# A decoder layer on one Trainium2 core: the last two pairs of feature tiles finish the tokens' second half first, the last norm and the stores of y go by halves, and the norm's columns and the operand loads are joined in

## The chip, the core and the metric

The kernel runs on one core of one Trainium2 chip. The metric is the device time of one execution in microseconds. Three executions of the kernel before took 2793.79, 2793.49 and 2789.72 us; the median is 2793.49.

In the tables PE is TensorE (PEld its weight loads), DVE is VectorE, ACT is ScalarE, POOL is GpSimd and SP is SyncE, which only issues DMAs. GpSimd and ScalarE issue DMAs too, each on a queue of its own.

## What is computed

One step of a hybrid decoder layer and the final norm. The part that matters here, cut from the reference:

```python
def block(x, rg_h, rg_conv, C, n, m, ml_conv, mk, mv, w):
    y, new = mixer(rmsnorm(x, w['g_mix']), rg_h, rg_conv, C, n, m, ml_conv, w)   # ends in y @ w_out
    x = x + y.astype(x.dtype)
    x = x + cross_attn(rmsnorm(x, w['g_xattn']), mk, mv, w).astype(x.dtype)      # q = h @ w_cq, ..., o @ w_co
    hf = rmsnorm(x, w['g_ffn'])
    x = x + (jnp.square(jax.nn.relu(hf @ w['w_up'])) @ w['w_down']).astype(x.dtype)
    return x, new

y_prompt = rmsnorm(xp, g_final)
y_sample = rmsnorm(xs, g_final)
```

x has 2048 features. 512 prompt tokens and 8 sampled tokens go through together, 520 in all. w_up is 2048 x 8192 and w_down 8192 x 2048. All is float32.

## The kernel before, in words

**Layout.** Features lie on the 128 partitions, so x is 16 feature tiles of 128 x 520. The tokens are cut into two halves of 260 (HALF, HT = 260). A matmul has a 128 x 128 block of weights and 260 tokens.

**Products.** Each operand is split into a high and a low part that TensorE multiplies exactly enough, and one product of parts is three matmuls (high by high, high by low, low by high). The projections w_out, w_cq, w_co, w_up and w_down are done by Strassen's scheme. A unit is a pair of feature tiles of the output, and its 2 x 2 blocks are (first or second tile) by (first or second token half). A unit takes seven products p0 to p6 of 24 matmuls each (`product`, L943, matmuls L955). Products go to three PSUM banks: p0, p2, p4 and p6 to acca, p1 and p5 to accc, p3 to accb. acca is carried on from p2 through p4 to p6. After each product VectorE adds the bank to a block of x (`onto`, L958, addition L962), or in the up stage ScalarE copies it out (L973) and VectorE adds (L971). The order of the blocks for p0 to p6 is (0,0), (1,1), (0,1), (0,0), (1,1), (0,1), (1,0): tile, then token half.

**Weights.** Raw weight blocks are loaded on SyncE's queue (`fetch`, L889, seven buffers) some products ahead. `prep` two products ahead (LOOK) forms sums of blocks on VectorE (L834), casts the high part on ScalarE (whi, L101) and takes the low part on VectorE (wlo, L102).

**Operands.** The right-hand sides are seven combinations of token data. They are built unit by unit at the end of the stage before (`mixed`), spilled to DRAM on GpSimd's queue (`spill`, L845: tdcq, tdup, tdd) and read back (`batch_load`, L856: the load L858 on SyncE's queue, the cast of the high part L859 on ScalarE, the low part L854 on VectorE). Each of the seven sets has two loads, of 520 KB and, for cq and up, 390 KB; the missing column block of these is built on chip (`set_tail`, L874).

**The stages in order.** Input projection and mixer, out (8 units), keys, cq (8), attention, co (8), up (32), then w_down in four groups d0 to d3 of 8 units each. x itself goes through DRAM between stages (dx_0 to dx_7 of four copies): co stores its x on GpSimd's queue (L995), up scales it back and stores it again (`scale_back`, L1323: loads L1341, multiplications L1345, stores L1346), and down loads it (`down_load`, L1362). In d3 all eight pairs stay in SBUF.

**scale_back.** Norm factors are kept apart from x. At the start of up they are inverted twice (`negative_inverse`, L1316: Ln on ScalarE, Exp, then two VectorE operations; each Ln and each Exp comes with a table load), and x is multiplied by the result.

**The last norm** (`final`, L1388). The squares of every x tile are summed into ss as the units of d3 end (L1385, L1386). After the last product, four matmuls by ones sum ss over the partitions, the factor r of all 520 tokens is computed over the full 128 x 520 (Ln, Exp, one correction step), and VectorE (L1413, eleven tiles) and GpSimd (L1411, five tiles, whose gain ScalarE multiplied in, L1392) multiply x by it. Sixteen stores of a full tile follow, alternately on the queues of SyncE and ScalarE (L1415).

**What sets the order.** A scheduler places the instructions of each engine by the order of the code and by priorities: the weight preparation and fetches have high priority, the evacuation of a product the next. Generators (`start`, `step_tasks`) advance by some steps with each product. In d3 the units run in order, but for 0 and 1, whose products alternate (`pairs`).

Of the kernel before, what the change touches and what calls it, by code (L numbers as in the profile page):

```python
# [17 lines left out]
P = 128  # L18
# [27 lines left out]
def tile_trunk(ctx: ExitStack, tc: tile.TileContext, a, o):  # L46
# [751 lines left out]
    def rest():  # L798
# [57 lines left out]
        def batch_load(key, s, b, n=4):  # L856
            hi, lo = op_tile(), op_tile()
            load(lo[:, 0:n].bitcast(F32), td[key][b][:, s, 0:n])  # L858
# [55 lines left out]
        def strassen(key, n, src, evac, enter_=None, leave=None, left=None, pairs=(), hooks={}):  # L914
# [12 lines left out]
            for u, p in order:  # L927
                k, box = base + u, boxes[u]
                job = dict(unit=k, q=p, kind=1, cost=0.55 if key == "cq" else 0.2, prep=lambda k=k, p=p: weights(k, p),
# [13 lines left out]
        def product(key, p, w, box):  # L943
            bank, _, s = ORDER[p]
            new = p in (0, 1, 3)
# [366 lines left out]
        def up_enter():  # L1312
            enter("d", x=2, r=1, t=2, w=2)()
            start(scale_back())
# [33 lines left out]
        def up_evac(u, p, box):  # L1348
# [11 lines left out]
        X = []  # L1360

# [8 lines left out]
        def down_evac(u, p, box, last):  # L1370
            onto([st["X", u][:, 0], st["X", u][:, 1]], p, box["out"])
            if p == 6 and not last:
                store(dx[3][u], st["X", u])
            if last and p == 6:
                for n in (2 * u, 2 * u + 1):
                    if n == 0:
                        st["sc2"] = op_tile((P, T), F32)
                        V.scalar_tensor_tensor(out=st["sc2"], in0=scl, scalar=1.0 / D, in1=scl,
                                               op0=ALU.mult, op1=ALU.mult)
                        st["ss"] = tl("ss", (P, T))  # L1380
                        S.activation(st["ss"], X[n], AF.Square)
                    else:
                        for c in HALF:
                            sq = ax()[:, 0:HT]
                            S.activation(sq, X[n][:, c], AF.Square)  # L1385
                            V.tensor_tensor(out=st["ss"][:, c], in0=sq, in1=st["ss"][:, c], op=ALU.add)  # L1386

        def final():  # L1388

            r, v, s_, q_ = (op_tile((P, T), F32) for _ in range(4))  # L1390
            for n in range(2, KB, 3):
                S.activation(X[n], X[n], AF.Copy, scale=pc(C_FIN, n))  # L1392
            for c in HALF:
# [263 lines left out]
```

## Time and profile before

| | us |
|---|---|
| median of three executions | 2793.49 |
| the profiled execution's own time | 2796.05 |
| its span | 2794.2 |
| last product of co ends, first product of up starts | 1409.9, 1411.7 |
| first unit of up ends | 1465.7 |
| last product of d3 ends | 2768.7 |
| first store of y issued | 2779.3 |

A time in the views is counted from the start of the span. A row of the timeline gives the start, the duration, the engine, the line of the code, the operation with its names (written by, read from), its shape and count, and in brackets how long the engine stood idle before it and what ended that. A group has the busy time, the mean of one in ns, and the idle time before. The table of windows gives for each stretch the busy time of each engine and in brackets the number of instructions.

### The profile page before, as it was taken

What the parts mean: (1) busy time and instruction counts of PE and PEld (TensorE: products, weight loads), DVE (VectorE), ACT (ScalarE), POOL (GpSimd) and SP (SyncE); (2) the same over time, 40 slices, a digit from 0 to 9 for tenths busy, and PEclk for the clock granted to TensorE, in tenths of its full rate; (3) what the DMA queues carried; (4) which work ended last, traced back from release to release, by engine and by line L of the source; (5) the groups of instructions that cost most, each with busy time, mean ns of one, the idle gap of its engine ahead of it and who ended that gap; (6) DMA issues with size and microseconds to landing.
All of it is one profiled execution on the core that took longest, in us unless ns stands there. A gap on an engine that the chain in (4) does not pass through costs nothing.

```text
span 2794.2 us, 52079 instructions
## 1 busy us (share of the span) xinstructions
PE 2665.4 (95%) x21146; PEld 2613.6 (94%) x21146; DVE 2245.1 (80%) x3203; ACT 1437.9 (51%) x2114; POOL 107.5 (4%) x164
## 2 busy tenths in 40 slices
PE   8999999999999999889969999999999999999996
PEld 8999999999999998669969999999998999999996
DVE  7777788658887898789878777777878887978886
ACT  6445556525455467675455455545554353434543
POOL 0000000030000000000000000000000000000000
PEclk9999999999999999999989999999999999999998
DMA  4666643377676579976666545454457465654632
GB/s 169 196 211 213 196 148 94 99 272 275 220 247 227 202 229 324 335 256 210 198 216 228 174 145 168 151 162 157 159 198 258 164 238 168 222 186 161 223 109 81
DMA packets 178857, 551.24 MB, mean 197 GB/s; under 512 B 23725, under 2 KB 33645, under 8 KB 178617
## 3 DMA queue, kind: packets, MB, share of 16 engines
q1 hardware_dynamic: 152808, 453.61, 48.9%
q0 software_dynamic: 24080, 90.50, 9.0%
q8 instruction: 166, 2.72, 0.4%
q10 hardware_dynamic: 1728, 3.80, 0.4%
q14 instruction: 75, 0.61, 0.1%
HBM read 427.45 MB, written 120.51 MB: 196 GB/s over the span
## 4 chain that ended last, share of the span: by engine, by line
PE 36%; issue 16%; DMA 4%; DVE 2%; ACT 2%; POOL 1%; SPq 0%; POOLq 0%; DVEq 0%; ACTq 0%
PE acca L955 19%; PE accc L955 9%; PE accb L955 5%; PE mv L1202 2%; PE ax L185 1%; DMA op<-dq 1%; DMA x<-dx 1%; DMA dx<-x 1%; DVE wlo L102 1%; DVE op L854 0%; DMA kv<-in_V 0%; ACT kv L1159 0%; PE row L1129 0%; DMA tdup<-w 0%; DMA op<-tdup 0%
## 5 line engine op out<-in xcount | busy, mean ns | idle before, releaser
L955 PE MATMUL acca<-op,whi 128*128 128x260 f32 x5632 | 1037.3, 285 | 33.2 <-ACT t L973 10.3
L955 PEld LDWEIGHTS acca<-op,whi 128*128 128x128 f32 x5632 | 877.7, 190 | 38.1 <-ACT whi L101 11.9
L955 PE MATMUL acca<-op,wlo 128*128 128x260 f32 x2816 | 801.9, 285 | 4.5 <-DVE wlo L102 4.4
L101 ACT CAST whi<-raw 128x1024 fp32r<-128x1024 f32 x388 | 406.8, 1050 | 426.7 <-PE acca L955 148.8
L955 PEld LDWEIGHTS acca<-op,wlo 128*128 128x128 f32 x2816 | 535.4, 190 | 6.1 <-DVE wlo L102 6.1
L102 DVE TENSOR_TENSOR wlo<-raw,whi 128x1024 fp32r<-128x1024 f32 x388 | 473.5, 1222 | 77.4 <-ACT whi L101 73.7
L955 PE MATMUL accc<-op,whi 128*128 128x260 f32 x2816 | 518.5, 284 | 1.4 <-ACT whi L101 1.3
L101 ACT CAST whi<-raws 128x1024 fp32r<-128x1024 f32 x264 | 276.9, 1049 | 369.2 <-PE accc L955 110.0
L166 PE MATMUL mm<-xa,whi 128*128 128x260 f32 x2624 | 432.9, 286 | 11.1 <-ACT whi L101 8.3
L955 PEld LDWEIGHTS accc<-op,whi 128*128 128x128 f32 x2816 | 438.1, 189 | 2.7 <-ACT whi L101 1.8
L102 DVE TENSOR_TENSOR wlo<-raws,whi 128x1024 fp32r<-128x1024 f32 x264 | 322.9, 1223 | 121.5 <-ACT whi L101 120.8
L955 PE MATMUL accc<-op,wlo 128*128 128x260 f32 x1408 | 400.2, 284 | 0.9 <-DVE wlo L102 0.9
L166 PEld LDWEIGHTS mm<-xa,whi 128*128 128x128 f32 x2624 | 365.0, 190 | 13.7 <-ACT whi L101 8.3
L955 PE MATMUL accb<-op,whi 128*128 128x260 f32 x1408 | 262.1, 286 | 8.4 <-ACT op L859 4.6
L955 PEld LDWEIGHTS accc<-op,wlo 128*128 128x128 f32 x1408 | 266.5, 189 | 1.3 <-DVE wlo L102 1.2
L166 PE MATMUL mm<-xa,wlo 128*128 128x260 f32 x1312 | 266.2, 284 | 0.0
L955 PEld LDWEIGHTS accb<-op,whi 128*128 128x128 f32 x1408 | 219.6, 190 | 9.8 <-ACT op L859 4.8
L166 PEld LDWEIGHTS mm<-xa,wlo 128*128 128x128 f32 x1312 | 203.9, 190 | 0.7 <-DVE wlo L102 0.5
L955 PE MATMUL accb<-op,wlo 128*128 128x260 f32 x704 | 200.8, 285 | 0.4 <-DVE wlo L102 0.3
L854 DVE TENSOR_TENSOR op<-op,op 128x1040 fp32r<-128x1040 f32 (+3 forms) x136 | 159.9, 1180 | 36.5 <-ACT op L859 22.0
L859 ACT CAST op<-op 128x1040 fp32r<-128x1040 f32 (+1 forms) x112 | 111.9, 1007 | 90.1 <-DMA op<-tdd 55.0
L101 ACT CAST whi<-wraw 128x1024 fp32r<-128x1024 f32 x82 | 85.5, 1043 | 122.8 <-PE mm L166 99.9
(386 smaller groups left out, 3355.0 us busy)
## 6 DMA issues: line engine op xcount, KB each, us to landing
raw<-in_w_up SPq DMA_DIRECT2D x128, 512.0 KB, 3.4
raw<-in_w_down SPq DMA_DIRECT2D x100, 512.0 KB, 4.1
wraw<-in_w_in SPq DMA_DIRECT2D x79, 512.0 KB, 4.0
tdd<-w POOLq DMA_DIRECT2D x32, 1040.0 KB, 6.3
x<-dx SPq DMA_DIRECT2D x56, 520.0 KB, 5.5
op<-tdd SPq DMA_DIRECT2D x56, 520.0 KB, 5.2
dx<-x POOLq DMA_DIRECT2D x48, 520.0 KB, 4.9
raw<-in_w_mk SPq DMA_DIRECT2D x32, 512.0 KB, 5.3
```

Source lines behind the costliest of these rows:

```text
L101: S.copy(hi, raw)
L102: V.tensor_tensor(out=lo, in0=raw, in1=hi.bitcast(F32), op=ALU.subtract)
L166: PE.matmul(ps[:, hf, 0:HT], w[:, j, :], x[:, HALF[hf]], start=(k == 0 and wi == 0), stop=(k == n - 1 and wi == 2))
L185: PE.matmul(out, u, v, start=first and i == 0, stop=last and i == 2)
L854: V.tensor_tensor(out=lo, in0=src, in1=hi.bitcast(F32), op=ALU.subtract)
L859: S.copy(hi[:, 0:n], lo[:, 0:n].bitcast(F32))
L955: PE.matmul(out, u[:, k], x[:, j], start=(new and k == 0 and i == 0), stop=(k == 7 and i == 2), skip_group_check=not new)
L1202: PE.matmul(st["mv"][i], x[:, ms], u[:, j], start=(k == 0 and wi == 0), stop=(k == KB - 1 and wi == 2))
```

## The change

The change has four parts.

1. `batch_load` issues the operand loads of cq and up on GpSimd's queue (store) in place of SyncE's (load).
2. `scale_back` is started after the last activation of unit 2 of up, in place of the stage's start; its first norm read (`mean_of`) still stands early.
3. In d3 the last two units (6 and 7) run p0, p1, p2, p4, p5 of each, then p3 of both, then p6 of both. With p5 the second token half of both units is complete. p6 gets a bank of its own, and what p4 had carried on into it is added to block (1,0) after p4. The fetch distances of these units follow.
4. The last norm runs by token halves (`final(1)` after p5 of unit 7, `final(0)` after its p6). The factor is computed on columns, tokens on partitions (`pieces`), with a square root in place of Ln and Exp; the columns of the scales are made after unit 0, where the table of the root is loaded too. Gains are multiplied in on ScalarE for units 0 to 5 (`gained`). Each half stores eight 128 x 2 x 260 pieces.

```diff
         def batch_load(key, s, b, n=4):
             hi, lo = op_tile(), op_tile()
-            load(lo[:, 0:n].bitcast(F32), td[key][b][:, s, 0:n])
+            (store if key in ("cq", "up") else load)(lo[:, 0:n].bitcast(F32), td[key][b][:, s, 0:n])
...
             for u in range(n):
-                if u in pairs:
+                if u == halves_:
+                    order += [(v, p) for v in (u, u + 1) for p in (0, 1, 2, 4, 5)]
+                    order += [(v, p) for p in (3, 6) for v in (u, u + 1)]
+                elif halves_ is not None and u == halves_ + 1:
+                    pass
+                elif u in pairs:
...
-            new = p in (0, 1, 3)
+            new = p in (0, 1, 3) or (p == 6 and "late" in box)
...
         def up_enter():
             enter("d", x=2, r=1, t=2, w=2)()
-            start(scale_back())
...
         def scale_back():
-            for _ in range(16):
-                yield
             va, vb = tl("x", (P, 2, T)), tl("x", (P, 2, T))
             v, y, t = va[:, 0], va[:, 1], vb[:, 0]
+            st["rphi"] = tl("r", (P, T))
+            with tc.issue_after(st["mark"].ins):
+                negative_inverse(y, t, scl)
             mean_of(v)
-            st["rphi"] = tl("r", (P, T))
-            negative_inverse(y, t, scl)
...
-                S.activation(w[:, 0:4], t, AF.Square)
+                ins = S.activation(w[:, 0:4], t, AF.Square)
+                if u == 2:
+                    st["mark"] = ins
+                    start(scale_back())
...
         def down_evac(u, p, box, last):
-            onto([st["X", u][:, 0], st["X", u][:, 1]], p, box["out"])
+            Xu = [st["X", u][:, 0], st["X", u][:, 1]]
+            onto(Xu, p, box["out"])
+            if p == 4 and "late" in box:
+                onto(Xu, 6, box["out"])
...
+            if last and p == 6 and u == 0:
+                ps = ax()
+                pieces(ps, [scl], ident, 0)
+                pieces(ps, [scl], ident, 1)
+                pieces(ps[:, 6:12], [esc], ident, 0)
+                pieces(ps[:, 6:12], [esc], ident, 1)
...
+                ins = S.activation(st["ss"], X[0], AF.Square)
+                with tc.issue_after(ins.ins):
+                    S.activation(cols[:, 3], ones[:, 0:6], AF.Sqrt)
+                square(Xu[1], HALF)
+                gained(u)
+            elif last and p == 6 and "late" not in box:
+                for x in Xu:
+                    square(x, HALF)
+                gained(u)
+            elif last and p == 5 and "late" in box:
+                for x in Xu:
+                    square(x, HALF[1:])
+                if u == 7:
+                    final(1)
+            elif last and p == 6:
+                square(Xu[0], HALF[:1])
+                if u == 7:
+                    sq = op_tile((P, HT), F32)
+                    S.activation(sq, Xu[1][:, HALF[0]], AF.Square)
+                    final(0, sq)
+                else:
+                    square(Xu[1], HALF[:1])
...
+        def pieces(ps, ts, col, h):
+            for c, cs in ((0, PIECES[0]), (1, PIECES[1]), (2, PIECES[0]), (2, PIECES[2])):
+                n = cs.stop - cs.start
+                for i, t in enumerate(ts):
+                    o_ = (h * HT if t.shape[-1] == T else 0) + cs.start
+                    PE.matmul(ps[0:n, 3 * h + c:3 * h + c + 1], t[:, o_:o_ + n], col[:, 0:1],
+                              start=(i == 0), stop=(i == len(ts) - 1))
+
+        def final(h, more=None):
+            c3 = slice(3 * h, 3 * h + 3)
+            v, s_, q_, rc = (cols[:, 3 + i, c3] for i in range(4))
+            ps = ax()
+            pieces(ps, [st["ss"]] + ([] if more is None else [more]), ones, h)
+            V.tensor_tensor(out=v, in0=ps[:, c3], in1=st["sc2"][:, c3], op=ALU.mult)
+            V.tensor_tensor(out=v, in0=v, in1=st["esc"][:, c3], op=ALU.add)
+            S.activation(s_, v, AF.Sqrt)
+            V.reciprocal(s_, s_)
...
+            rp = ax()[:, 0:HT]
+            for c, cs in enumerate(PIECES):
+                n = cs.stop - cs.start
+                PE.matmul(rp[:, cs], rc[0:n, c:c + 1].to_broadcast([n, P]), ident[0:n, 0:n],
+                          start=True, stop=True)
+            r = op_tile((P, HT), F32)
+            S.copy(r, rp)
+            for i, u in enumerate((1, 0, 3, 2, 5, 4, 6, 7)):
+                x = st["X", u][:, :, HALF[h]]
+                if u > 5:
+                    for j in range(2):
+                        V.scalar_tensor_tensor(out=x[:, j], in0=x[:, j], scalar=pc(C_FIN, 2 * u + j), in1=rp,
                                                op0=ALU.mult, op1=ALU.mult)
+                elif u % 2:
+                    V.tensor_tensor(out=x, in0=x, in1=rp[:, None, :].to_broadcast([P, 2, HT]), op=ALU.mult)
+                else:
+                    G.tensor_tensor(out=x, in0=x, in1=r[:, None, :].to_broadcast([P, 2, HT]), op=ALU.mult)
+                (S.dma_start if i % 2 else load)(o["y"][2 * u:2 * u + 2, :, HALF[h]].rearrange("n p t -> p n t"), x)
...
-                     pairs=(0,) if last else (0, 6),
+                     pairs=(0,) if last else (0, 6), halves_=6 if last else None,
...
-        final()
         stage["stack"].close()
+        axs.close()
```

Three places show how the instructions move. The first is the start of the up stage. On SyncE's queue before, loads of raw weights (raw, from w_up) and of operands (op, from tdup) stand in turn, and x of `scale_back` follows:

```order
L889 DMA raw_16546<-in_w_up 128x1024
L858 DMA op_16334<-tdup_120 128x1040
L858 DMA op_16339<-tdup_121 128x780
L889 DMA raw_16607<-in_w_up 128x1024
L858 DMA op_16373<-tdup_120 128x1040
L858 DMA op_16378<-tdup_121 128x780
L858 DMA op_16412<-tdup_120 128x1040
L889 DMA raw_16736<-in_w_up 128x1024
L858 DMA op_16417<-tdup_121 128x780
L858 DMA op_16464<-tdup_120 128x1040
L858 DMA op_16469<-tdup_121 128x780
L1341 DMA x_17310<-dx_0_146 128x1040
```

On GpSimd's queue now, the operand loads stand behind the last spill of w and the store of dx_7, the last x of co:

```order
L1004 DMA dx_6_152<-x_15971 128x1040
L845 DMA tdup_121<-w_16159 1024x1x260
L858 DMA op_16213<-tdup_121 128x780
L858 DMA op_16252<-tdup_120 128x1040
L858 DMA op_16257<-tdup_121 128x780
L858 DMA op_16291<-tdup_120 128x1040
L1004 DMA dx_7_153<-x_16204 128x1040
L858 DMA op_16296<-tdup_121 128x780
L858 DMA op_16334<-tdup_120 128x1040
L858 DMA op_16339<-tdup_121 128x780
L858 DMA op_16373<-tdup_120 128x1040
L858 DMA op_16378<-tdup_121 128x780
```

SyncE's queue holds raw weights alone there; the eight x loads of `scale_back` (now L1348) stand between raw loads of units 3 to 6.

The second place is ScalarE at the start of up: before, the two table loads and activations of the first inverse stand among the operand casts, and the same four rows come again after the last of these casts.

```order
L874 CAST op_16295<-w_16452 128x260
L1318 ACT_TABLE_LOAD
L1318 ACTIVATE x_17036<-scl 128x520
L1319 ACT_TABLE_LOAD
L1319 ACTIVATE x_17036<-x_17036 128x520
L101 CAST whi_16513<-raws_16421 128x1024
L859 CAST op_16295<-op_16296 128x780
```

Now both stand among the weight casts (whi) of unit 3; the copies t (now L982) take products out of PSUM:

```order
L101 CAST whi_17239<-raw_17061 128x1024
L1326 ACT_TABLE_LOAD
L1326 ACTIVATE x_17198<-scl 128x520
L1327 ACT_TABLE_LOAD
L1327 ACTIVATE x_17198<-x_17198 128x520
L101 CAST whi_17274<-raw_16998 128x1024
L982 COPY t_17233<-accc_17248 128x260
L101 CAST whi_17306<-raws_17152 128x1024
L982 COPY t_17233<-acca_17208 128x260
L101 CAST whi_17336<-raw_17000 128x1024
L1326 ACT_TABLE_LOAD
```

The third place is ScalarE at the end: od holds the norm's columns, ax_31221 the factor of the second half, L1428 and L1420 are squares of x, and L1478 the stores of y.

```order
L101 CAST whi_31275<-raw_30918 128x1024
L1454 ACTIVATE od<-od 128x3
L1428 ACTIVATE ax_31331<-x_30775 128x260
L1467 COPY op_31225<-ax_31221 128x260
L1478 DMA out_y<-x_29386 128x2x260
L1478 DMA out_y<-x_29776 128x2x260
L1478 DMA out_y<-x_30307 128x2x260
L1478 DMA out_y<-x_30980 128x2x260
L1428 ACTIVATE ax_31334<-x_30775 128x260
L1428 ACTIVATE ax_31363<-x_30980 128x260
L1420 ACTIVATE op_31366<-x_30980 128x260
L1454 ACTIVATE od<-od 128x3
```

The four stores of the second half stand ahead of the last three squares of the first. On TensorE the four column matmuls of the second half stand behind the third matmul of p3 of unit 7, and its three broadcasts behind the first matmul of p6 of unit 6; the eight and three of the first half come last.

More of the change, by code (lines that the diff above doesn't have):

```diff
@@ L928, in strassen @@
                 k, box = base + u, boxes[u]
-                job = dict(unit=k, q=p, kind=1, cost=0.55 if key == "cq" else 0.2, prep=lambda k=k, p=p: weights(k, p),
+                late = halves_ is not None and u >= halves_
+                if p == 0 and late:
+                    box["late"] = True
+                job = dict(unit=k, q=p, kind=1, late=late, far=5 if late and u > halves_ else 7, cost=0.55 if key == "cq" else 0.2, prep=lambda k=k, p=p: weights(k, p),
                            run=lambda w, p=p, box=box: product(key, p, w, box),
@@ new lines, in square, with gained @@
+        def square(x, cs):
+            for c in cs:
+                sq = ax()[:, 0:HT]
+                S.activation(sq, x[:, c], AF.Square)
+                V.tensor_tensor(out=st["ss"][:, c], in0=sq, in1=st["ss"][:, c], op=ALU.add)
+        def gained(u):
+            for n in (2 * u, 2 * u + 1):
+                S.activation(X[n], X[n], AF.Copy, scale=pc(C_FIN, n))
+        PIECES = [slice(0, CH), slice(CH, 2 * CH), slice(2 * CH, HT)]
+        def pieces(ps, ts, col, h):
[5 more added lines that the diff above has]
+                              start=(i == 0), stop=(i == len(ts) - 1))
@@ L1494, in rest @@
         NEED = (0, 1, 1, 3)
+        LATE = (0, 1, 1, 5)
         fetches = [[] for _ in seq]
```

58 lines of the change are left out of this document (15 added, 43 removed).

## The prediction, made before the changed kernel ran

> **What bounds the kernel now.** I read the page first, then busy time by stretches of 10 to 20 us, then the timeline and the chain of waits wherever TensorE stood still.
>
> ```profile
> span 2794.2 us, 52079 instructions
> PE 2665.4 (95%) x21146; PEld 2613.6 (94%) x21146; DVE 2245.1 (80%) x3203; ACT 1437.9 (51%) x2114; POOL 107.5 (4%) x164
> ```
>
> TensorE is busy for 95% of the span, so an edit beside its work is worth nothing, and only the places where it waits can give time. Two of these lie in the change's reach: the start of the up stage and the end. Here are stretches of the windows view: width, then busy time of PE, PEld, DVE, ACT and POOL, granted clock, DMA share, GB/s. The first is a steady co unit, the next five the start of up, the last the stores of y.
>
> ```profile
> 1340.00:1360.00 20.00, 20.00 (x169) 20.00 (x168) 17.55 (x23) 9.67 (x11) 1.41 (x2) 1.00 0.63 200
> 1410.00:1420.00 10.00, 7.07 (x56) 6.87 (x57) 9.80 (x14) 8.34 (x13) 0.55 (x1) 1.00 0.74 293
> 1420.00:1430.00 10.00, 4.50 (x26) 3.75 (x26) 8.15 (x10) 9.45 (x12) 0.00 (x0) 0.85 0.40 146
> 1430.00:1440.00 10.00, 5.35 (x23) 5.05 (x23) 8.97 (x12) 4.24 (x6) 0.00 (x0) 0.63 0.55 199
> 1440.00:1450.00 10.00, 2.96 (x13) 2.97 (x14) 7.86 (x12) 5.64 (x10) 0.00 (x0) 0.54 0.50 186
> 1450.00:1461.00 11.00, 7.92 (x62) 7.52 (x60) 5.66 (x9) 5.25 (x6) 0.54 (x1) 0.96 0.42 146
> 2780.00:2794.20 14.20, 0.00 (x0) 0.00 (x0) 5.91 (x9) 0.00 (x0) 4.21 (x4) 0.50 0.80 300
> ```
>
> From 1410 to 1461 VectorE is the busiest engine (40.4 of 51 us, the five windows added), and it has holes of its own. What made them stands in the timelines and the chain. The first two rows are TensorE's last matmul of co and its longest stall; then SyncE's queue, ScalarE and VectorE; the last three, without a queue's name, are links of the chain.
>
> ```profile
> 1409.60 0.28 PE L955 MATMUL accc<-op,wlo 128*128 128x260 f32 x1
> 1447.04 0.80 PE L955 MATMUL acca<-op,whi 128*128 128x260 f32 x2 [10.08 <-ACT t L973]
> 1439.15 0.33 SPq L889 DMA_DIRECT2D raw<-in_w_up  x1
> 1439.58 1.33 SPq L858 DMA_DIRECT2D op<-tdup  x3
> 1443.71 0.84 ACT L859 CAST op<-op 128x780 fp32r<-128x780 f32 x1 [3.52 <-DMA op<-tdup]
> 1448.02 1.28 ACT L1318 ACT_TABLE_LOAD   x1
> 1449.31 0.64 ACT L1318 ACTIVATE x<-x 128x520 f32<-128x520 f32 x1
> 1458.55 2.04 DVE L1345 TENSOR_TENSOR x<-x,r 128x520 f32<-128x520 f32 x3 [3.30 <-DMA x<-dx]
> 1440.06 5.26 DMA op<-tdup
> 1453.40 5.12 DMA x<-dx
> 1460.98 4.68 PE acca L955 x24
> ```
>
> The last three operand loads stand on SyncE's queue behind a weight load (raw, L889) that waited for a free buffer until 1439.15; they were issued from 1439.58 and the last landed at 1445.3. ScalarE's casts waited for them, the copy t (L973) waited behind the casts, and TensorE waited 10.08 us for that copy. Then the last product waited for a VectorE addition queued behind L1345, which waited 5.12 us for x<-dx. The first unit of up thus ran from 1409.9 to 1465.7, 56 us; the steady row above has 20.00 of 20 us busy with 169 matmuls, and a unit is seven products of 24 matmuls: about 20 us, 2.9 a product. Some 36 us are lost here.
>
> The tail, from the timeline:
>
> ```profile
> 2768.75 0.43 DVE L962 TENSOR_TENSOR x<-acca,x 128x260 f32<-128x260 f32 x1 [1.56 <-PE acca L955]
> 2769.21 0.70 ACT L1385 ACTIVATE ax<-x 128x260 f32<-128x260 f32 x2 [1.72 <-DVE x L962]
> 2770.12 1.15 PE L1395 MATMUL ax<-ss,ones 128*128 128x260 f32 x4 [1.41 <-DVE ss L1386]
> 2773.15 1.28 ACT L1399 ACT_TABLE_LOAD   x1
> 2777.86 0.60 ACT L1407 COPY rp<-op 128x520 f32<-128x520 f32 x1 [2.11 <-DVE op L1403]
> 2777.97 6.25 POOL L1411 TENSOR_TENSOR x<-x,op 128x520 f32<-128x520 f32 x5 [175.28 <-DVE op L1403]
> 2778.49 7.42 DVE L1413 SCALAR_TENSOR_TENSOR x<-x,par,rp 128x520 f32<-128x520 f32 x11 [0.66 <-ACT rp L1407]
> 2779.27 9.41 SPq L1415 DMA_DIRECT2D out_y<-x  x8
> ```
>
> The last product ends at 2768.7 and the span at 2794.2: 25.5 us with TensorE out of work. Nine of them are one serial chain over all 520 tokens, and from the first store at 2779.27 on it is 15.0 us of stores. By the window of 2780 the stores moved 300 GB/s over 14.2 us, all 4.26 MB of y, with the DMA engines busy 0.80 of it, 11.4 us.
>
> **The change part by part.** Durations are of the profiled execution, which took 2796.05 us; the median shown is 2793.49, 2.56 less, and I take that off at the end.
>
> *Operand loads of up on GpSimd's queue, and scale_back moved to units 3 to 6.* Both act at the start of up, so they go together. There the loads no longer stand behind the weight loads. They stand behind the store of dx_7, and nine of the fourteen come after it.
>
> ```profile
> 1417.03 0.55 POOL L995 DMA_DIRECT2D dx<-x  x1 [19.41 <-DVE x L962]
> 752.49 0.55 POOL L995 DMA_DIRECT2D dx<-x  x1 [17.00 <-DVE x L962]
> 754.91 0.87 POOL L845 DMA_DIRECT2D tdcq<-w  x1 [1.87 <-DVE w L834]
> dx<-x POOLq DMA_DIRECT2D x2, 520.0 KB, 4.9
> tdcq<-w POOLq DMA_DIRECT2D x1, 1040.0 KB, 6.6
> ```
>
> An issue of 520 KB takes GpSimd 0.55 us, so the nine are issued from 1417.6 to 1422.5. The queue does not wait for a landing: the spill of 754.91 was issued 2.4 us after a store that takes 4.9. Four loads of 520 KB and five of 390 (the casts' 780 columns) are 4.1 MB; at the 300 GB/s of the y stores that is 14 us, so the last lands near 1434 in place of 1445.3. VectorE then sets the pace. Of its 40.4 us the moved scale_back goes:
>
> ```profile
> L1345 DVE TENSOR_TENSOR x<-x,r 128x520 f32<-128x520 f32 x4 | 2.7, 697 | 3.3 <-DMA x<-dx 3.3
> L1321 DVE SCALAR_TENSOR_TENSOR x<-x,x 128x520 f32<-128x520 f32 x2 | 1.4, 700 | 0.1
> ```
>
> With four more operations of that shape (L1320 twice, L1332, L1335) that is 2.7 + 1.4 + 2.8 = 6.9 us, which leaves 33.5. Without a hole the work that ended at 1461 ends at 1443.5, 17.5 us earlier. I leave 3 us of holes: 14.5. At most it is 19, where the last product also runs in 2.9 in place of its 4.68. If the loads land no earlier than now, only what follows 1447.0 shrinks: five products at 2.9 end at 1461.5 in place of 1465.7, 4 us. So -14.5, from -4 to -19.
>
> In units 3 to 6 the moved work comes back beside full products: two groups of two table loads and two activations on ScalarE (2 x 1.28 + 2 x 0.64 = 3.84 us each), six small-norm operations and sixteen multiplications by 0.70 on VectorE, eight loads x<-dx on SyncE ahead of weight loads. The steady row shows ScalarE idle for half of the time and VectorE for 2.4 us in 20, so most hides. Weights are prepared two products ahead, 5.8 us, which covers 3.84. Without cover it costs what the row of 1458.55 shows, 3.3 us for a wait. Before, the same multiplications in units 1 and 2 cost TensorE about 2 us. I set the balance at 0, from -2 to +5.
>
> *Operand loads of cq on GpSimd's queue.* The waits view over 835 to 925:
>
> ```profile
> ACT op L859 <- DMA op<-tdcq: 5.1, 2, 4.5
> ```
>
> These 5.1 us of ScalarE are the most that can go; TensorE has mk products to do beside them. The last load now stands behind two memsets on GpSimd. So -2, from -4 to +3.
>
> *The norm's columns after unit 0 of d3.* Sixteen matmuls of one column, two VectorE operations, one table load hidden on the half-idle ScalarE; seven more multiplications by the gain beside products.
>
> ```profile
> 838.55 3.33 PE L257 MATMUL ax<-ones,ss 128*128 128x1 f32 x24 [2.06 <-DVE ss L1002]
> L1091 DVE RECIPROCAL su<-su 128x1 f32<-128x1 f32 x16 | 2.5, 157 | 1.4 <-ACT op L1090 1.2
> ```
>
> 3.33 / 24 = 0.14 each: 2.2 us at most, half of it if they run faster between full products. So +1.5, from +1 to +2.2.
>
> *The tail.* The second token half is complete four products (11.5 us) before the end. Its norm, seven multiplications and eight stores run beside these products. They put four small matmuls and three broadcasts into TensorE (0.6 + 0.6 us) and I allow 0.5 for their waits. Behind the last product the first half is left: addition 0.43; square 0.35; eight small matmuls 1.1; eight column operations on VectorE at 0.16, 1.3; a root on ScalarE, between 0.16 and the 0.64 of a full activation, 0.2 taken as it has three columns; three broadcasts 0.6 (bounds 3 x 0.14 and 3 x 0.29, L1395's rate); seven handovers of 0.05. That is 4.3. The first multiplication (0.67) gives a store at 5.0. Before, 15.0 us passed from the first store to the end, 11.4 of it transfers; half the bytes make 5.7, and the 3.6 around them stay: 14.3. GpSimd agrees: copy of r by 4.8, three multiplications of 1.25, last store at 8.6, and 5.5 until the end. So -25.5 + 14.3 + 1.7 = -9.5, from -6 to -12.5; the poor end is a transfer that the halved rows make slower, or ScalarE's queue (below).
>
> Sum: -14.5 + 0 - 2 + 1.5 - 9.5 = -24.5, so 2771.5 against the profiled 2796.05, and 2769 against the median.
>
> **The rivals.**
>
> *Loads late on GpSimd's queue.* The store of dx_7 holds nine loads until 1417.6, and the DMA share is 0.74 there. If they land no earlier than now, up gives -4 in place of -14.5: 2780. For it: the queue order. Against it: SyncE issued its last three 17 us later than GpSimd will. Chance 0.17. A rule of the Trainium skill bears on this (SBUF — State Buffer, section "SBUF: two separate sides", and "Who interferes with whom"): descriptors of a GpSimd-issued DMA need a port that a VectorE copy in a two-port mode locks, and such a DMA took 3.1 us in place of 0.62, so such transfers belong on another queue. By its figures nine loads would be issued over an estimated 28 us and this rival would hold, 2780. The page adds that tensor_tensor has no such mode; the issue rows above, 0.55 and 0.87 us beside a VectorE that the steady row shows 88% busy, agree, and the chance stays.
>
> *The moved norm stalls units 3 to 6.* Eight x loads land late one by one, each holding VectorE's weight splits 3.3 us less the 2.4 of slack, and both ScalarE groups 2 us over their cover: +7 + 4, in place of 0: 2780. Before shows two such waits for x<-dx, hence 0.10.
>
> *ScalarE's stores hold the last norm.* Four issues of half 1 stand ahead of the last squares on ScalarE, and three wait for GpSimd's multiplications (1.25 each). The broadcasts stand behind the first matmul of the last product but one, 5.7 us before the end; the copy follows, and GpSimd is done about 1.2 us before the last product. If GpSimd takes twice its 3.75 us, the last square waits 2.5 us and the norm with it: 2772. Chance 0.07, inside the forecast's range.
>
> *Slower: GpSimd's queue moves one load at a time.* If each load waits for the landing of the one before (4.9 us), nine take 44 us and the last lands at 1461.7, 16 us later than now: up +16, and cq with thirteen such loads some +10, total +18: 2811. It decides from about 4 us a load, (1453.5 - 1417.6) / 9, where up's loss eats the tail's gain. Against it stands the pair at 752 and 754. Chance 0.05.
>
> **How the numbers follow.** Forecast 2762 to 2777: 0.55, with the third rival 0.62. The terms' poor ends add to no change at all, the good ones to 2757. The two at 2780: 0.27, together or worse near 2789: 0.04 of these. More than forecast, 2752 to 2761, all terms near their good ends: 0.06. Slower: 0.05. The range 2758 to 2786 leaves out about 0.13. A difference of 0.2% (5.6 us) is about what a measurement tells from none. Faster by more: 0.91; within: 0.04; slower: 0.05.
>
> **What would show it.** Right: no TensorE gap over 5 us between 1410 and 1450, op<-tdup issued by GpSimd from 1417 on and landed by 1436; VectorE busy over 9 of 10 us there; units 3 to 6 of up at 20.2 to 21 us; half of the y stores landed before the last product plus 3 us; 14 us from the last product to the end. Wrong: GpSimd issues of 3 us, waits for x<-dx of over 3 us in units 3 to 6, a squaring behind out_y on ScalarE, or stores of y below 300 GB/s.

## The result, and the profile after

The changed kernel took 2772.30 us, the median of five executions (2771.25 to 2774.59). Five executions of the kernel before have the median 2790.53. The ratio is 0.9943, with a 95% interval from 0.9928 to 0.9958. In a later job, beside other executions of the kernel before, the ratio was 0.9959 (0.9944 to 0.9974). By these two ratios the change saves 16 and 11 us (the two medians lie 18.2 us apart; the ratio and its interval count here). The prediction was 2769 us, 24.5 less than before: the sign was right, and the gain was half to two thirds of what was forecast.

The page of the changed kernel:

```profile
span 2769.5 us, 52212 instructions
PE 2671.0 (96%) x21210; PEld 2618.1 (95%) x21210; DVE 2240.5 (81%) x3216; ACT 1440.7 (52%) x2121; POOL 123.9 (4%) x193
```

Its span is 24.7 us below that of before, almost the forecast sum. A third of that is chance, as the stages below show. The table gives the time between fixed marks of one profiled execution of each kernel, in us: cq from the first matmul of mk to the first of mv; start of up from the store of x by co's first unit to the activation that closes up's first unit; units 1 and 2, and units 3 to 8, between these activations; d0 to d2 from up's last such activation to the last store of x in d2; d3 to the last product's end; the tail from there. The kernels e1 to e11 are the experiments below.

| kernel | cq | start of up | units 1, 2 | units 3 to 8 | d0 to d2 | d3 | tail |
|---|---|---|---|---|---|---|---|
| before | 450.3 | 192.5 | 43.0 | 121.0 | 508.0 | 166.6 | 25.5 |
| changed | 445.4 | 183.5 | 40.3 | 127.1 | 499.7 | 169.9 | 16.6 |
| changed again (e9) | 446.4 | 183.2 | 40.3 | 128.7 | 506.0 | 169.5 | 17.5 |
| e1, loads alone | 446.9 | 188.4 | 45.5 | 121.0 | 506.5 | 165.0 | 25.3 |
| e2, scale_back alone | 453.7 | 184.1 | 40.3 | 128.0 | 502.9 | 165.6 | 25.5 |
| e3, d3 and the norm alone | 449.1 | 191.9 | 42.9 | 121.0 | 501.9 | 168.1 | 17.2 |
| e4, loads and scale_back | 445.1 | 183.4 | 40.3 | 127.9 | 504.4 | 165.7 | 25.3 |
| e5, x spread out | 447.6 | 185.5 | 40.3 | 121.9 | 509.5 | 168.5 | 16.8 |
| e6, stores on SyncE | 447.0 | 184.5 | 40.3 | 127.0 | 502.9 | 168.2 | 15.5 |
| e7, splits put off | 448.6 | 181.1 | 40.4 | 128.5 | 504.4 | 168.6 | 16.8 |
| e8, e5 to e7 together | 447.4 | 181.1 | 40.4 | 121.9 | 504.6 | 170.5 | 15.1 |
| e10, the same again | 447.1 | 180.9 | 40.4 | 121.9 | 503.9 | 168.1 | 15.8 |
| e11, d3's order kept | 448.2 | 183.1 | 40.3 | 128.8 | 505.6 | 165.6 | 24.2 |

The column d0 to d2 runs from 499.7 to 509.5. All that the change moved there are the column matmuls of part 4, with two small operations of VectorE. They do not run after unit 0 of d3, where the code has them: they need none of d3's results, and the scheduler put them at the start of d0 (timeline of the changed kernel):

```profile
2085.36 1.72 PE L1443 MATMUL ax<-ident,scl 128*128 128x1 f32 x16
2087.02 1.83 PE L1443 MATMUL ax<-ident,esc 128*128 128x1 f32 x16
2088.89 0.17 DVE L1398 COPY od<-ax 128x12 f32<-128x12 f32 x1 [2.75 <-PE ax L1443]
```

VectorE waits 2.75 us for them, and the first matmuls of d0 come some 3 us later. But 30 us on nothing of it is left: the 169th matmul of a product after up's last Relu starts 30.2 to 30.8 us after it in the nine kernels with the columns, and 29.8 to 30.5 (once 34.2) in the four without. From there to the last store of x in d2 the order of instructions is the same in all 13 kernels, and yet the time runs from 469.2 to 479.0. The profile of before stands near the slow end (478.0) and that of the changed kernel at the fast end (469.2), while the same kernel took 475.7 in e9. So 8 of the 24.7 us are nothing that the change did. The other columns are tighter, and they carry the rest of this text. By them the change is: cq -4.1 (the mean of the ten kernels with the new loads against the three without), start of up -8.9, units 1 and 2 -2.7, units 3 to 8 +7.2 (the changed kernel, e9 and e11), d3 +3.2 (the mean of eight kernels with the new order against five without), the tail -8.4 (the mean of the five with the new tail unedited against the four without). That is -13.7, which agrees with the two timed ratios.

The start of up in the changed kernel, in the windows view (columns as before):

```profile
1410.00:1420.00 10.00, 8.58 (x61) 8.14 (x60) 8.77 (x13) 5.97 (x9) 5.17 (x10) 0.95 0.54 184
1420.00:1430.00 10.00, 6.32 (x24) 5.42 (x25) 9.97 (x14) 5.07 (x6) 0.12 (x1) 0.56 0.96 387
1430.00:1440.00 10.00, 4.48 (x21) 4.17 (x21) 9.46 (x12) 6.66 (x11) 0.00 (x0) 0.67 0.16 53
1440.00:1447.00 7.00, 7.00 (x51) 6.82 (x51) 1.62 (x2) 1.83 (x3) 0.00 (x0) 0.88 0.19 61
```

The loads come in one burst (0.96 of the DMA engines, 387 GB/s), and VectorE has hardly a hole left from 1420 to 1440 (9.97 and 9.46 of 10 us busy), as was forecast. But TensorE is not done when VectorE is. The timeline shows why:

```profile
1413.68 4.21 POOL L858 DMA_DIRECT2D op<-tdup  x8
1431.04 1.04 ACT L101 CAST whi<-raws 128x1024 fp32r<-128x1024 f32 x1 [3.96 <-PE accb L964]
1434.31 1.79 ACT L859 CAST op<-op 128x780 fp32r<-128x780 f32 x2
1436.32 0.36 ACT L982 COPY t<-acca 128x260 f32<-128x260 f32 x1
1438.68 0.96 DVE L854 TENSOR_TENSOR op<-op,op 128x780 fp32r<-128x780 f32 x1
1436.74 0.80 PE L964 MATMUL acca<-op,whi 128*128 128x260 f32 x2 [5.52 <-ACT t L982]
```

p2 adds onto p0's bank, so it needs the copy t of p0. That copy still stands on ScalarE behind the operand casts, and these behind a weight cast that waited 3.96 us for p3 (accb). p2 starts at 1436.7, and p2, p5, p4 and p6, 14.4 us, come after it. The last operand split on VectorE ends at 1439.6, and the unit at 1451.

In units 3 to 6 the waits that came back (timeline, the chain's two DMA links, then the group of `scale_back`'s sixteen multiplications):

```profile
1538.37 1.31 DVE L1352 TENSOR_TENSOR x<-x,r 128x520 f32<-128x520 f32 x2 [4.12 <-DMA x<-dx]
1540.87 0.39 PE L964 MATMUL acca<-op,wlo 128*128 128x260 f32 x1 [1.81 <-DVE wlo L102]
1529.12 5.53 DMA dx<-x
1534.71 3.56 DMA x<-dx
L1352 DVE TENSOR_TENSOR x<-x,r 128x520 f32<-128x520 f32 x16 | 10.7, 696 | 8.2 <-DMA x<-dx 8.2
```

x has two buffers. A load of x waits for a store of x to land (5.53 us), then takes 3.56 itself; the multiplication waits for it at the head of VectorE's queue, the next weight split (L102) stands behind, and TensorE stops for 1.8 us. The same happens once more at 1560.8, with a wait of 3.79 us.

The tail, after the last product's end at 2752.8:

```profile
2747.50 3.85 POOL L1477 TENSOR_TENSOR x<-x,op 128x520 f32<-128x520 f32 x3 [164.05 <-ACT op L1467]
2748.84 3.80 ACTq L1478 DMA_DIRECT2D out_y<-x  x4
2752.69 0.70 ACT L1428 ACTIVATE ax<-x 128x260 f32<-128x260 f32 x2 [5.27 <-issue]
2753.11 0.43 DVE L1429 TENSOR_TENSOR ss<-ax,ss 128x260 f32<-128x260 f32 x1 [1.83 <-ACT ax L1428]
2754.36 0.35 PE L1443 MATMUL ax<-ones,ss 128*128 128x1 f32 x2 [1.52 <-DVE ss L1429]
2757.78 1.71 PE L1464 MATMUL ax<-ident,od 128*128 128x128 f32 x6 [1.78 <-DVE od L1459]
2759.93 1.91 DVE L1475 TENSOR_TENSOR x<-x,ax 128x520 f32<-128x520 f32 x3 [2.30 <-ACT op L1467]
```

ScalarE's four stores of the second half (ACTq) wait for GpSimd's multiplications and are through at 2752.64; the squares that the last norm needs start at 2752.69, and VectorE waited for them. From the first multiplication on it is 9.5 us, near the 10 of the forecast; up to it 7.1 us passed, in place of 4.3.

### The profile page after: what moved, and what is told of

It reads as the page before. It is cut to its first block, busy times and chain, and to the rows that moved or that the text cites. A ratio compares the mean times of both kernels' runs of the same rounds, so it can differ in the third digit from the quotient of the medians.

```text
span 2769.5 us, 52212 instructions
## 1 busy us (share of the span) xinstructions
PE 2671.0 (96%) x21210; PEld 2618.1 (95%) x21210; DVE 2240.5 (81%) x3216; ACT 1440.7 (52%) x2121; POOL 123.9 (4%) x193
## 4 chain that ended last, share of the span: by engine, by line
PE 54%; issue 26%; DVE 8%; DMA 6%; ACT 4%; POOL 1%; SPq 0%; POOLq 0%; ACTq 0%; DVEq 0%
PE acca L964 21%; PE accc L964 10%; PE mm L166 10%; PE accb L964 6%; DVE wlo L102 2%; PE mv L1211 2%; PE mk L1191 2%; PE ax L185 1%; ACT whi L101 1%; DMA op<-dq 1%; DVE op L854 1%; DMA ct<-in_C 1%; PE aux L185 1%; DMA x<-dx 1%; DMA dx<-x 1%
## 5 line engine op out<-in xcount | busy, mean ns | idle before, releaser
L102 DVE TENSOR_TENSOR wlo<-raw,whi 128x1024 fp32r<-128x1024 f32 x388 | 473.0, 1220 | 72.5 <-ACT whi L101 68.5
L102 DVE TENSOR_TENSOR wlo<-raws,whi 128x1024 fp32r<-128x1024 f32 x264 | 322.6, 1222 | 116.7 <-ACT whi L101 115.9
```

Of the source, the lines that this page charges most:

```text
L102: V.tensor_tensor(out=lo, in0=raw, in1=hi.bitcast(F32), op=ALU.subtract)
```

## The experiments

**Each part alone.** The first job took the change apart: e1 has only the edit of `batch_load`, e2 only `scale_back` behind unit 2, e3 all the rest, and e4 the first two together.

```diff
e1  -            load(lo[:, 0:n].bitcast(F32), td[key][b][:, s, 0:n])
    +            (store if key in ("cq", "up") else load)(lo[:, 0:n].bitcast(F32), td[key][b][:, s, 0:n])
e2  -            start(scale_back())
    +                if u == 2:
    +                    st["mark"] = ins
    +                    start(scale_back())
```

> Only the operand loads of cq and up go on GpSimd's queue; all else as before. Theory (each part adds on its own): the cq stage gains the 4.4 us that the two profiles differ by up to the start of mv, and at up's start the last load lands some 10 us earlier, so TensorE's longest stall (10.1 us before) shrinks; but the table loads and the waits for x<-dx of scale_back stay behind it. Time -8 us, and the first unit of up takes 50 us in place of 56. Rival (scale_back is what the start of up waits for): no more than -5, all of it in cq, and the first unit stays at 55 to 56 us.

> Only scale_back is started behind unit 2 of up; loads, tail and last norm as before. Theory (each part adds): the last loads still land around 1445, so the first unit of up gains 4 us (the wait for x<-dx and the second pair of table loads), unit 2 gains 2, and units 3 to 6 lose the 6 us that they lost in the changed kernel: time 0, within 2 us. Rival (scale_back is what the start waits for): the first unit gains 10 us or more, time -5 or less.

> Only d3's order, the columns and the last norm by halves; loads and scale_back as before. Theory: d3 costs 3 us more and the end from the last product on 16.6 in place of 25.5 us, as in the changed kernel: time -5.5 us. Rival (the 9 us by which the two profiles differ at the starts of d0 to d2, where no instruction moved, come from this part): -14.

> Both edits of the up stage and cq, the end as before. Theory (parts add): -10.5 us, which with the end's -5.5 makes the -16 measured; the first unit of up takes 47 us as in the changed kernel. Rival (the two edits of up need each other): the time of this one is below the sum of the first two runs by 3 us or more.

The ratios to the kernel before were 0.9971 (0.9956 to 0.9986) for e1, 0.9973 (0.9955 to 0.9991) for e2, 0.9959 (0.9943 to 0.9975) for e3 and 0.9966 (0.9951 to 0.9981) for e4. These intervals are 8 to 10 us wide, too wide to add or subtract parts, so the stages decide.

e1 took cq down by 4 and the start of up by 4, and lost 2.5 in units 1 and 2. Up's first unit, from co's last product on, took 51.4 us, near the 50 of its theory and not the 55 of its rival. e2 alone took 8.4 from the start of up, twice what its theory gave and nearly what its rival asked for, with the loads still on SyncE; its time, -7.5 us, goes with the rival. e4 has both. Its first unit takes 46.4 us where 47 was expected, but its start of up is only 0.7 below that of e2. So the parts neither add nor need each other: **scale_back's place is worth 8 us there, and the loads, once it is gone, less than 1**, which is within the spread of that column (183.1 to 185.5 among the six kernels with both edits and the old splits). Cut at two points, co's last store of x and the start of p2, the start of up shows why:

| us | co's first to last store | to the start of p2 | to the unit's closing activation |
|---|---|---|---|
| before | 143.4 | 30.0 | 19.0 |
| e1, loads alone | 144.0 | 25.4 | 19.0 |
| e2, scale_back alone | 143.2 | 27.2 | 13.7 |
| changed | 145.2 | 23.6 | 14.7 |

Both edits bring p2 forward, and only scale_back's shortens what follows it. The first row here is e1's p2 (timeline); the others are from e2, SyncE's queue and TensorE in the timeline, and a window:

```profile
1436.31 0.80 PE L955 MATMUL acca<-op,whi 128*128 128x260 f32 x2 [6.55 <-ACT t L973]
1436.91 1.33 SPq L858 DMA_DIRECT2D op<-tdup  x3
1444.47 0.80 PE L955 MATMUL acca<-op,whi 128*128 128x260 f32 x2 [10.28 <-ACT t L973]
1450.00:1457.00 7.00, 7.00 (x59) 6.83 (x58) 4.23 (x5) 2.23 (x3) 0.00 (x0) 1.00 0.24 77
```

In e2 the three last loads are issued 2.7 us sooner than before (1436.91 against 1439.58), and p2 waits as long (10.28 against 10.08). Of the 8.4 us, 2.8 come ahead of p2 and 5.3 behind it: from 1450 on TensorE works without a stop, at full clock, where before the last product waited for x<-dx and took 4.68 us. In the changed kernel p2 starts another 3.6 us sooner after co's last store, but what follows takes 1 us longer, and so do co's last units, by some 2 us: co's stores span 144.0 to 147.4 us in the ten kernels with the new loads and 143.2 to 143.4 in the three without. That co's additions wait on VectorE behind the earlier splits is the likely reason; no run shows it.

In cq the loads matter. Before, TensorE waited there twice for VectorE's multiplication that empties the bank of mk (L1188), which the waits view (835 to 925) lists in the first row; the other two are from the changed kernel, mk's only wait there and ScalarE's wait for the loads:

```profile
PE mk L1182 <- DVE sq L1188: 4.0, 2, 2.6
PE mk L1191 <- DVE op L854: 1.0, 1, 1.0
ACT op L859 <- DMA op<-tdcq: 4.1, 1, 4.1
```

The first wait stands in the lists of all three kernels with loads on SyncE's queue (4.0 to 4.4 us) and in none of the ten others.

e3 confirms tail and d3 by stage (-8.3 and about +2.4), in sum -6. Its timed -11.5 (-7 to -16) is more than that, and agrees with the rival's -14; but the rival put the difference into d0 to d2, and that column spreads over 10 us among kernels that are alike there. What the timed excess is stays open.

**x of scale_back spread out (e5).** On the changed kernel, each load and multiplication is held behind a unit of its own.

```diff
             for u in range(KB // 2):
-                for _ in range(6):
-                    yield
+                m = st["mark"]
+                while st["mark"] is m:
+                    yield
+                m = st["mark"]
                 x = tl("x", (P, 2, T))
-                load(x, dx[2][u])
-                for _ in range(6):
-                    yield
-                for i in range(2):
-                    V.tensor_tensor(out=x[:, i], in0=x[:, i], in1=st["rphi"], op=ALU.mult)
+                with tc.issue_after(st["sp"].ins):
+                    load(x, dx[2][u])
+                while st["mark"] is m:
+                    yield
+                with tc.issue_after(st["dve"].ins):
+                    for i in range(2):
+                        V.tensor_tensor(out=x[:, i], in0=x[:, i], in1=st["rphi"], op=ALU.mult)
```

> The changed kernel, but each load of x and each pair of multiplications of scale_back is held behind a unit of its own (one x in some two units, from unit 4 on); the two inverses stay in unit 3. Theory (units 3 to 6 lose 6 us because x has two buffers, so a load waits for the store of x two places before, and the multiplication holds the next weight split on VectorE): from the end of unit 2 to that of unit 6 it takes 81 to 82 us in place of 86.8, time 5 us below the changed kernel's. Rival (the loss comes from the two inverses with their table loads on ScalarE): 86 us as now, time 0 to -1.

Units 3 to 8 took 121.9 us in place of 127.1, 5.2 less, and from the end of unit 2 to that of unit 6 it is 81.6 us, as the theory had it. The group of the multiplications in e5, and one window:

```profile
L1356 DVE TENSOR_TENSOR x<-x,r 128x520 f32<-128x520 f32 x16 | 10.4, 692 | 0.0
1533.00:1553.00 20.00, 20.00 (x169) 20.00 (x169) 16.34 (x19) 10.38 (x13) 1.40 (x2) 1.00 0.61 212
```

The idle time ahead of them, 8.2 us in the changed kernel, is 0.0. The two inverses with their table loads are where they were, so the loss was the wait for x; to the tables no more is left than the 0.9 us by which e5 stays above the 121.0 of before. The time, 0.9930 (0.9911 to 0.9950) of before, is not to be told from the changed kernel's.

**The second half's stores on SyncE (e6).**

```diff
-                (S.dma_start if i % 2 else load)(o["y"]...)
+                (S.dma_start if i % 2 and h == 0 else load)(o["y"]...)
```

> The changed kernel, but all eight stores of the second half are issued by SyncE, none by ScalarE. Theory (the last squares of the first half wait on ScalarE behind stores that wait for GpSimd): the squares come 1.1 us earlier, and from the last product to the end it takes 15.5 us in place of 16.6. Rival (the queue for the stores is what ends last, so an earlier norm meets stores that are still moving): 16.6 as now.

The tail is 15.5 us against 16.6. In e6's timeline the squares start right after VectorE's addition, and only the last of them waits for the last product:

```profile
2751.35 0.70 ACT L1428 ACTIVATE ax<-x 128x260 f32<-128x260 f32 x2 [3.89 <-DVE x L971]
2753.37 0.42 ACT L1420 ACTIVATE op<-x 128x260 f32<-128x260 f32 x1 [1.32 <-DVE x L971]
```

So the stores on ScalarE held the norm, by 1.1 us; the three tails with this edit (15.1 to 15.8) lie below all five without it (16.6 to 17.5). The timed ratio, 0.9937 (0.9919 to 0.9956), cannot tell that.

**The last operand splits put off (e7).** In `batch_load` cast and low part of up's last three sets become a function that is called after p0, p1 and p2 of unit 0.

```diff
+            if key == "up" and s in SLOT_OF[4:]:
+                splits.append(split)
+            else:
+                split()
...
+                        **{(0, p): lambda: (splits.pop(0)(), splits.pop(0)()) for p in (0, 1, 2)}})
```

> The changed kernel, but up's last three operand sets are split (cast and low part) after unit 0's p0, p1 and p2 in the order of the code, so that fewer casts stand ahead of the copies t on ScalarE. Theory A (TensorE's p2 waits for a copy that is only queued behind casts): the stall of 5.9 us before p2 shrinks to 2 or less, the first unit from the store of x by co's last unit takes 32 to 35 us in place of 38.3, time -4 to -6 against the changed kernel. Theory B (VectorE's low parts of the operands bound the unit): p2 starts earlier, but p4 to p6 wait as long; 37 to 38.3 us, time 0 to -1.

Co's last store to the end of unit 0 took 35.0 us against 38.3 (37.4 in e9; 37.1 to 38.9 in all six kernels without this edit, 35.6 and 35.9 in e8 and e10), 2.4 to 3.3 less: more than theory B allowed, at the weak end of A, and the wait ahead of p2 fell from 5.5 to 3.2 us where A asked for 2. Five casts now stand behind the copy, and it still waits:

```profile
1434.40 1.04 ACT L101 CAST whi<-raws 128x1024 fp32r<-128x1024 f32 x1 [5.52 <-PE accb L970]
1437.24 0.36 ACT L988 COPY t<-acca 128x260 f32<-128x260 f32 x1
1437.65 0.80 PE L970 MATMUL acca<-op,whi 128*128 128x260 f32 x2 [3.18 <-ACT t L988]
```

The deferred casts were 2.3 us of its wait. Ahead of the copy still stands the weight cast, which waits 5.52 us until p3 is done, and p3 runs ahead of p2. As long as it stands there the copy cannot come earlier; an order without it was not tried. The time, 0.9946 (0.9927 to 0.9964), shows no difference.

**All three together (e8), and again beside the changed kernel (e9, e10).**

> The three edits of the last runs together on the changed kernel. If each removes a stall of its own place, the sum: -10 to -12 us against the changed kernel, about 2761. Under the three rivals: no more than -2.

> The changed kernel once more, on the same chip as the next two, for the comparison and for the spread of its stages. 0.994 of the kernel before, as first measured; the stages in which no instruction moved (d0 to d2) may differ from the first profile by some us either way, the moved ones by less than 2.

> The version with the three edits of the second round (x of scale_back spread over units, stores of the second half all on SyncE's queue, the last three operand sets split behind p0 to p2) once more. If its stages add as its first profile shows (5 in units 3 to 6, 1 to 1.5 at the end, 3 in the first unit of up), it is 8 to 10 us below the changed kernel of the same job, 0.9965 to 0.997 of it; if it is within 4 us, the gains of the stages do not reach the time.

e8 gave 0.9922 (0.9898 to 0.9946), about 6 us below the changed kernel's first ratio and short of the -10; the two intervals overlap. In the job with both, the changed kernel had 0.9959 (0.9944 to 0.9974) and e10 0.9912 (0.9894 to 0.9931), 2779.79 and 2764.71 us: 13 us by the ratios, 15 by the medians, and the intervals do not meet. By stages e10 gains 2.3 at the start of up, 6.8 in units 3 to 8 and 1.7 at the end against e9, 10.8 us, where 8 to 10 was expected. This version beats both kernels. In e9 the stages that the change moved lie within 1.6 us of the first profile, as expected.

**d3's old order with the new norm (e11).** Units 6 and 7 run their products in turn, and both halves of the norm come after the last product.

```diff
+            elif last and p == 6:
+                for x in Xu:
+                    square(x, HALF)
+                if u < 6:
+                    gained(u)
+                if u == 7:
+                    final(1)
+                    final(0)
...
-                     pairs=(0,) if last else (0, 6), halves_=6 if last else None,
+                     pairs=(0,) if last else (0, 6), halves_=None,
```

> The changed kernel with d3's old order: units 6 and 7 run p0 to p6 in turn, and both halves of the last norm and all stores come after the last product; the columns, the root and the joined stores stay. Theory (most of the end's gain comes from half the stores lying beside the products): from the last product to the end 22 to 23 us in place of 16.6, d3 2 us shorter, time 3.5 to 4.5 us above the changed kernel. Rival (the gain comes from the short norm on columns): the end 18 to 19 us, time equal to the changed kernel's or below it.

The tail is 24.2 us, 1.2 below the kernels without the change, and d3 takes 165.6, as they do. The halves thus buy 6.7 to 7.6 us at the end, and the norm on columns, run twice in a row, 1.2. Their price is 3.0 us: the last fourteen products of d3 take 43.5 us in each of the eight kernels with the new order and 40.5 in each of the five without. By the stages the theory holds. Its time, 3.5 to 4.5 us above the changed kernel, is not shown: 0.9952 (0.9935 to 0.9969) is not to be told from 0.9959. The first multiplications of the two halves in e11's timeline show the short norm stretched by two chains in a row, 8.0 us after the last product's end at 2757.9 and again 6.7 us later:

```profile
2765.89 1.90 DVE L1466 TENSOR_TENSOR x<-x,ax 128x520 f32<-128x520 f32 x3
2772.54 1.91 DVE L1466 TENSOR_TENSOR x<-x,ax 128x520 f32<-128x520 f32 x3 [2.30 <-ACT op L1458]
```

## Why the prediction was right, and where it was wrong

The time lies in the range, and the change is faster, as forecast. That 2772.30 is within 4 us of 2769 is in part luck. The executions of the changed kernel came out low: by the stages it should take 2780 us, and in the later job the same kernel had the median 2779.79, above the 2762 to 2777 that had the best chance. The sum was too large by some 11 us:

| term | forecast | by the stages |
|---|---|---|
| start of up | -14.5 (-4 to -19) | -8.9 |
| balance of units 1 and 2 and 3 to 6 | 0 (-2 to +5) | -2.7 + 7.2 = +4.5 |
| cq | -2 (-4 to +3) | -4.1 |
| columns after unit 0 of d3 | +1.5 | 0 (they ran at the start of d0) |
| products and halves in d3 | +1.7 | +3.2 |
| tail | -11.2 | -8.4 |

**Start of up.** The failed step is "VectorE then sets the pace ... the work that ended at 1461 ends at 1443.5". The splits did go without a hole, and the loads did come early. But the addition that ended at 1461 before was not the last of the splits; it was that of p4's bank, which only p6 waited for, and behind the copy that starts p2 lie four products. (Where the prediction counts five products after 1447.0, p3 had already run; in e2 the four took 13.7 us.) I counted the engine that is busiest and did not follow the order of the copy on ScalarE, though the quoted row of 1447.04 names it. e7 shows that 2.4 to 3.3 us of that order can be had. The two edits were put down together, and the text set the loads first. The runs show the opposite: e2 alone brings 8.4 of the 8.9, where the prediction gave 4 us to a kernel whose loads land no earlier.

**Units 3 to 6.** The step "the steady row shows ScalarE idle for half of the time and VectorE for 2.4 us in 20, so most hides" counted engine time. What was short was a buffer: waits of 4.12 and 3.79 us for x<-dx at the head of VectorE's queue. The rival "the moved norm stalls units 3 to 6" named this wait and gave it 0.10; it happened at two thirds of its +11, and by e5 almost without the ScalarE part of it.

**cq.** The sign was right, but by another wait than the one quoted. Of the 5.1 us for which ScalarE waited for the loads, 4.1 are still there in the changed kernel. What went is TensorE's own wait of 4.0 us for the bank of mk. How the loads' queue brought that multiplication forward on VectorE stays open.

**Columns.** That they cost nothing is luck: the prediction looked for them beside full products of d3, and they ran at the start of d0, where the delay that their 3.5 us brought was made up within 30 us.

**The tail.** The chain to the first multiplication took 7.1 us in place of 4.3. The step "3.33 / 24 = 0.14 each" is off by two: that row's 24 records are 12 matmuls of float32, which show as two records each. So eight small matmuls took 1.65 us in place of 1.1, and three broadcasts, at a granted clock of 0.50, 1.71 in place of 0.6; that is 1.7 us. The other 1.1 is the third rival, ScalarE's stores ahead of the last squares (e6). It came without the condition set for it: GpSimd took 3.85 us and not twice 3.75, and the last two issues took the 1.3 us behind it. The part from the first multiplication on was right, 9.5 against 10. In d3 the same two records make 0.95 and 0.92 us (the two rows, from the changed kernel) of what was put at 0.6 and 0.6. With two delays of 0.4 us each ahead of p5's first low parts that is 2.7 of the 3.0 us.

```profile
2742.46 0.95 PE L1443 MATMUL ax<-ones,ss 128*128 128x1 f32 x8
2746.09 0.92 PE L1464 MATMUL ax<-ident,od 128*128 128x128 f32 x6
```

Of the signs that the prediction named, the loads and VectorE did as it said. Against it stood a TensorE gap of 5.52 us before 1450, units 3 to 6 at 21.7 us each, the two waits for x<-dx of over 3 us, and the squares behind out_y on ScalarE.

The slower rival, GpSimd's queue moving one load at a time, did not occur: eight loads were issued in 4.21 us and moved at 387 GB/s. That is 0.53 us an issue beside a VectorE that was busy 8.8 of 10 us, as in the rows of before. The exception for tensor_tensor that the prediction took from the Trainium skill (SBUF — State Buffer, section "Who interferes with whom") agrees with this trace.

## What to carry to other kernels

When a stage starts with a pile of preparation, follow the instruction that releases the waiting engine through every in-order queue that it stands in; the busiest engine may be done long before. When work is moved into a steady stretch, count the buffers and the landing times between its own steps as well as the free time of the engines, and hold it back until the data have surely landed. Look in the trace for where the scheduler put new instructions; the place in the code need not be it. Before a difference of one profile is put down to a change, compare a stage in which nothing moved.

## What the runs showed of the hardware that was not expected

A float32 matmul shows as two records: four column matmuls of the changed kernel stand as eight records in 0.95 us, so 0.24 us a matmul beside full products. A stretch with the same instructions in the same order differed by up to 9.8 us between executions (d0 to d2 behind their first 30 us, 469.2 to 479.0; 6.5 of it between two executions of one kernel), which is more than most parts of this change are worth. The stores of y in pieces of 260 columns moved at 330 to 360 GB/s in most slices of the DMA view, against 376 to 393 for the full rows of before.
